# Thirty-two bytes further per k-tile: where x^T and the activations lie in SBUF, against the weight tiles

## The chip, the cores and the metric

One NeuronCore of one Trainium2 chip runs the kernel. The metric is the device time of one execution in microseconds; the median of three runs is used.

## The reference

Two transformer blocks run one after the other on 256 tokens of width 2048, all in float32. What matters here is that almost all the work lies in products of 256 token rows with large weight matrices:

```python
def first_block(x, ...):
    h = rmsnorm(x, pre_mix_g);  proj = h @ w_in            # 2048 x 4368
    ...                                                    # windowed and forgetting attention
    x = x + rmsnorm(concat([o_a, o_b]) @ w_out, post_mix_g)
    h = rmsnorm(x, pre_ffn_g);  u = causal_dwconv(h @ w_up, conv_w, conv_b)   # 2048 x 11264
    gate, val = split(u)
    return x + rmsnorm((gelu(gate) * val) @ w_down, post_ffn_g)               # 5632 x 2048

def second_block(x, c, ctx, ...):
    sh_a, sc_a, g_a, sh_m, sc_m, g_m = split(silu(c) @ w_ada + b_ada)
    ...                                                    # attention over latents and context, pooling
    x = x + g_a * (concat([attn, pool]) @ w_out)
    hm = modulate(rms_norm(x, norm_mlp_w), sh_m, sc_m)
    x = x + g_m * (square(relu(hm @ w_mlp_up)) @ w_mlp_down)                  # 2048 x 8192 x 2048
    return rms_norm(x, final_norm_w)
```

## The kernel before

Every large product is a `Group`: its weights stream from HBM in blocks of two 128-row tiles of 1024 columns (1 MB), and x^T stays in SBUF. To keep float32 accuracy, each operand is split into a high part and the rest, and each product of tiles is made of three matmuls, wh·xh, wh·xl and wl·xh (`products`, L273 to L286). ScalarE makes the high weights from the raw block (L156) and VectorE the low ones (L168), one tile of each for every 128 rows.

There are two layouts. In a feature-major product ("A": up, mup, qk, qa, q, kva, part of ckv and kv) the weight tile is the stationary operand, 128 columns at a time, and x^T of one k-tile (128 features by 256 tokens) moves. In a token-major product ("B": mdn, dn, wo_a, wo_b, wo_p, u, v) x^T of one k-tile and one token tile is stationary, and the weights move, 512 columns at a time. Names in the profile: `b_up` is the PSUM bank of an up product, `hi` and `lo` are weight tiles, `a` and `p` are x^T or activations out of the pools `a8` and `p4`.

`run` (L121 to L266) goes through the blocks in order. For each k-tile (a "unit") it issues all column tiles of that k-tile: 8 column tiles by 3 matmuls, 24, in an A product, and 4 banks by 3, 12, in a B product. The last block of a group goes bank by bank instead, alternating between its two k-tiles. So inside a unit the k-tile of x and the pair of weight buffers stay the same.

The tiles come from pools. The pool `w` has four buffers for high weights and four for low ones, 1040 columns (4160 bytes) each, used in turn. 4160 is 16·256 + 64, so the four buffers start at different places modulo 256 bytes: in the built program at 192, 0, 64 and 128, the high and the low tile of a unit alike. Pool `a8` (8 buffers of 8192 bytes) holds x^T, eight k-tiles of 256 columns per buffer (`make_ht`, L340 on), and pool `p4` (9 buffers of 4096 bytes) holds the activations of the feed-forwards, four k-tiles per buffer (L954 and L1334). A k-tile is 1024 bytes, so every k-tile starts at 192 modulo 256. Column offsets inside a weight tile are multiples of 512 bytes. The start of SBUF is taken by a scratch of 16384 bytes for DMA descriptors.

```python
            passes = ((wh, xh), (wh, xl), (wl, xh))
            for m, (ww, xx) in enumerate(passes):
                if op[0] == "A":
                    _, o, c = op
                    dst, lhsT, rhs = bank[:, o:o + 256], ww[:, c:c + 128], xx
                else:
                    _, o, w_, tt, c = op
                    dst, lhsT, rhs = bank[:, o:o + w_], xx[:, 128 * tt:128 * tt + 128], ww[:, c:c + w_]
```

Of the kernel before, what the change touches and what calls it, by code (L numbers as in the profile page):

```python
# [15 lines left out]
T = 256  # L16
# [5 lines left out]
# columns of the packed per-feature vectors  # L22
# [9 lines left out]
# when the adaptive modulation takes a step, by product: every so many ticks (99: never), or at these ticks  # L32
# [4 lines left out]
# products without a reader while the norms before these products run  # L37
# [3 lines left out]
class Group:  # L41
    """One weight-streaming product: blocks of two 128-row weight tiles against a resident x^T."""
# [10 lines left out]
def a_banks(nf, col0=0):  # L53
    """Feature-major results: two 128-feature tiles of 256 tokens per bank."""
    return [[("A", 256 * j, col0 + 128 * (i + j)) for j in range(min(2, nf - i))] for i in range(0, nf, 2)]


def b_banks(widths, col0=0):
    """Token-major results: one bank per token tile and column chunk."""
    out = []  # L60
    for tt in range(2):
        c = col0
        for n in widths:
            out.append([("B", 0, n, tt, c)])
            c += n
    return out


class Kernel:
# [51 lines left out]
    def run(self, groups):  # L121
# [26 lines left out]
        def hi_to(j):  # L148
            while len(his) <= min(j, 2 * len(blocks) - 1):
                dma_to(len(his) // 2 + 2)  # L150
                views, raw, w = part(len(his))
                self.n += 1
                hi = self.w_p.tile([128, 1040], F32R, tag="hi", name=f"hi{self.n}")[:, :w]
                with self.behind("hi"):
                    for h, r in views(hi, raw):
                        nc.scalar.copy(h, r)  # L156
                his.append(hi)

        def lo_to(j):
            while len(los) <= min(j, 2 * len(blocks) - 1):  # L160
                n = len(los)
                hi_to(n)
                views, raw, w = part(n)
                self.n += 1
                lo = self.w_p.tile([128, 1040], F32R, tag="lo", name=f"lo{self.n}")[:, :w]
                with self.behind("lo"):
                    for (l, r), (h, _) in zip(views(lo, raw), views(his[n], raw)):
                        self.dve.tensor_tensor(out=l, in0=r, in1=h.bitcast(F32), op=ALU.subtract)  # L168
                los.append(lo)

        banks = None
        for i, (g, b) in enumerate(blocks):
# [40 lines left out]
            if g.tail and b == g.nb - 2:  # L213
                # the first token tile's results come before the second's
                w2 = []
                for u in range(4):
                    lo_to(2 * i + u)
                    hi_to(2 * i + 3)
                    w2.append((his[2 * i + u], los[2 * i + u]))
                    for n in range(nb // 2):  # L220
                        unit(banks[n], g.banks[n], u)
                    self.tick(False)
                for n in range(nb):
                    if n >= nb // 2:
                        for u in range(4):
                            unit(banks[n], g.banks[n], u)
                    mm = self.mm
                    g.done(n, banks[n])
                continue
# [38 lines left out]
    def behind(self, kind):  # L268
        """Issue order after an instruction of a norm that the next products wait for."""
        q = self.held[kind]  # L270
        return self.tc.issue_after(q.pop(0).ins) if q else nullcontext()
# [31 lines left out]
    def later(self, *steps, every=1):  # L303
        """Run steps one by one at coming ticks."""
        def gen():
            for f in steps:
                for _ in range(every):
                    yield
                f()
        self.sides.append(gen())  # L310

    def keep_warm(self, n, after=None, rhs=None):
        """Products without a reader, so that the tensor engine's clock stays up while it would wait."""
# [6 lines left out]
    def preload(self, func, after):  # L320
        """Has the scalar engine load the table of a function ahead of its use."""
# [9 lines left out]
    def loader(self, w, k0, c0, n):  # L331
        """Blocks of two k-tiles from row k0 and columns c0:c0+n."""
# [7 lines left out]
    def make_ht(self, src, gain, shift=None):  # L340
        """src(tt, k) -> token-major [128, 128]; gain, shift: per-feature columns."""
# [4 lines left out]
        def emit(i):  # L346
            if len(his) <= i // 4:
                his.append(self.A8([128, 8, 256], F32R))
                los.append(self.A8([128, 8, 256], F32R))
# [32 lines left out]
        def head(tt):  # L382
            """The first four k-tiles of one token tile."""
            if not his:
                his.append(self.A8([128, 8, 256], F32R))
                los.append(self.A8([128, 8, 256], F32R))
# [15 lines left out]
    def rstd(self, parts, n):  # L402
        """(mean of squares + eps) ** -0.5 from partial sums [128, m]."""
# [14 lines left out]
    def scale_rows(self, x, ss, n=D, out=None, first=False):  # L418
        """x * rstd for a token tile; the first of two on one engine, else shared by two."""
# [12 lines left out]
    def row(self, src):  # L432
        """A vector of D on every partition, in two tiles; returns columns of it."""
# [6 lines left out]
    def attn1(self, jobs, v_of, evac, bias, sink):  # L440
        """jobs: (q, k, j, half, head). Yields once per head."""
# [87 lines left out]
    def o_evac(self, his, los, gain, acc, base=0):  # L529
        """o^T of a head pair: times the group's gain, split, and its squares summed."""  # L530
# [16 lines left out]
    def token_rstd(self, acc, n):  # L547
        """rstd per token [128, 2] from squares summed feature-major [128, 256]."""
# [49 lines left out]
    def row_of(self, cols, tile_=None):  # L598
        """A [128, 2048] tile whose every row is the vector held in columns [128, 16]."""
# [13 lines left out]
    def main(self):  # L613
# [15 lines left out]
        heads = self.const("heads", [128, 48])  # L629
# [29 lines left out]
        # x^T of the first block, one token tile after the other  # L659
# [19 lines left out]
        def silu_rows():  # L679
            """silu of c and c_ctx, each along every partition's row."""  # L680
# [18 lines left out]
        # -- v and forget gates, token-major  # L699
# [63 lines left out]
        # -- k and v of the windowed heads  # L763
# [16 lines left out]
        # -- q of the windowed heads, heads j and j + 8 in one tile  # L780
# [19 lines left out]
        # -- q and k of the forgetting heads, with the windowed attention beside them  # L800
# [27 lines left out]
        # -- output projection: windowed heads, then forgetting heads  # L828
        w_out = a["w_out"]

        def pair_rows(w, r0, n, c0):
            """Rows of k-tile j: 64 of head j, 64 of head j + n, among 2n heads from row r0."""
# [28 lines left out]
        def residual(y, x, r):  # L861
            """x += y * r for one token tile; returns the squares' sums of the new x."""
# [8 lines left out]
        def add_norm(n, half, y, hold):  # L871
            """One result chunk of y: its squares, its gain, and then x += norm(y) and y = norm(x)."""
# [44 lines left out]
        # -- residual + norm, then x^T of the next product  # L917
# [6 lines left out]
        # -- first feed-forward  # L924
        gs = {}

        def up(g):
            def after(banks):
# [23 lines left out]
                def split(i):  # L952
                    if i == 0:
                        out[:] = [self.P4([128, 4, 256], F32R) for _ in range(2)]  # L954
# [49 lines left out]
        # context: norm, modulation and its x^T beside the last products  # L1004
# [39 lines left out]
        # -- second block: context keys and values  # L1044
# [9 lines left out]
        def split(x, his, lo):  # L1054
            """hi + lo of x [128, 512], hi by partition halves in two tiles."""
# [5 lines left out]
        def twice(c):  # L1061
            """The high parts of the keys in the other partition half too."""
# [6 lines left out]
        # -- second block: projections of the latent tokens  # L1069
# [20 lines left out]
        def rope(x, his, lo):  # L1090
            """Rotated x [128, 512] (features on partitions, 256 tokens twice), as hi (by halves in two tiles) + lo."""
# [33 lines left out]
        # -- attention over the latent window and the context  # L1125
        def attn2():
            # per half s of the heads: high parts in their own partitions, low parts in the other half
# [141 lines left out]
        # -- output projection of the second block: x += g_a * (...)  # L1269
# [51 lines left out]
        # -- second feed-forward  # L1321
# [6 lines left out]
        def up2(g):  # L1328
            def after(banks):
                gs[g] = hi, lo = [], []  # L1330

                def split(i):
                    if i % 2 == 0:
                        hi.append(self.P4([128, 4, 256], F32R))  # L1334
                        lo.append(self.P4([128, 4, 256], F32R))
# [13 lines left out]
        def finish(n, half):  # L1349
            """The gain of one chunk of the last norm, and the norm when a token tile is complete."""  # L1350
# [77 lines left out]
def arrays(inp):  # L1428
    """The inputs as the program takes them, and constants that depend on shapes alone."""
# [10 lines left out]
    # the two halves of w's columns c0:c1, side by side by 512  # L1440
# [59 lines left out]
```

## Time and profile before

| | |
|---|---|
| median of 3 runs | 2159.97 us (2158.24 to 2160.66) |
| span of the profiled execution | 2159.2 us |
| TensorE busy, matmuls | 2134.7 us, 99% |
| TensorE busy, weight loads | 1926.6 us, 89% |
| VectorE busy | 1578.7 us, 73% |
| ScalarE busy | 1076.4 us, 50% |
| HBM read | 484.90 MB, 226 GB/s over the span |

The span runs from the first to the last instruction of one profiled execution; its own time is that span, 0.8 us under the median of the other runs. Busy times of different engines overlap. Matmul records overlap one another too, since a matmul is issued while the one before it is still draining; the pace of TensorE is the distance between two starts.

### The profile page before, as it was taken

What the parts mean: (1) busy time and instruction counts of PE and PEld (TensorE: products, weight loads), DVE (VectorE), ACT (ScalarE), POOL (GpSimd) and SP (SyncE); (2) the same over time, 40 slices, a digit from 0 to 9 for tenths busy, and PEclk for the clock granted to TensorE, in tenths of its full rate; (3) what the DMA queues carried; (4) which work ended last, traced back from release to release, by engine and by line L of the source; (5) the groups of instructions that cost most, each with busy time, mean ns of one, the idle gap of its engine ahead of it and who ended that gap; (6) DMA issues with size and microseconds to landing.
All of it is one profiled execution on the core that took longest, in us unless ns stands there. A gap on an engine that the chain in (4) does not pass through costs nothing.

```text
span 2159.2 us, 35018 instructions
## 1 busy us (share of the span) xinstructions
PE 2134.7 (99%) x14342; PEld 1926.6 (89%) x14342; DVE 1578.7 (73%) x2094; ACT 1076.4 (50%) x1557; POOL 38.3 (2%) x58
## 2 busy tenths in 40 slices
PE   8999999999999999999999999999999999999998
PEld 7988877999998999989889878889898998989986
DVE  6777688888689787887899777765656657555476
ACT  5456565555454543544666466354543434434343
POOL 0001010000000000000000000000000000000000
PEclk9999999999999999999999999999999999999999
DMA  8753675667767788787878744855767677565572
GB/s 309 262 191 123 157 230 218 231 244 248 254 216 254 252 298 309 273 310 255 307 259 287 247 139 156 196 175 177 252 200 270 215 246 243 191 194 179 194 233 98
DMA packets 120640, 490.86 MB, mean 227 GB/s; under 512 B 8672, under 2 KB 12576, under 8 KB 107040
## 3 DMA queue, kind: packets, MB, share of 16 engines
q1 hardware_dynamic: 120480, 488.63, 67.0%
q8 instruction: 112, 1.84, 0.3%
q14 instruction: 48, 0.39, 0.0%
HBM read 484.90 MB, written 2.13 MB: 226 GB/s over the span
## 4 chain that ended last, share of the span: by engine, by line
PE 95%; DVE 2%; ACT 1%; DMA 1%; POOL 0%; issue 0%; POOLq 0%; ACTq 0%; SPq 0%; DVEq 0%
PE b_up L285 23%; PE b_mup L285 17%; PE b_mdn L285 16%; PE b_dn L285 11%; PE b_qk L285 4%; PE b_wo_a L285 4%; PE b_u L285 2%; PE b_v L285 2%; PE b_wo_p L285 2%; PE b_qa L285 2%; PE b_q L285 2%; PE b_wo_b L285 2%; PE b_aux L1156 1%; PE b_aux L1199 1%; PE b_aux L1185 1%; PE b_aux L495 1%
## 5 line engine op out<-in xcount | busy, mean ns | idle before, releaser
L168 DVE TENSOR_TENSOR lo<-raw,hi 128x1024 fp32r<-128x1024 f32 (+2 forms) x716 | 850.0, 1198 | 445.7 <-ACT hi L156 444.2
L156 ACT CAST hi<-raw 128x1024 fp32r<-128x1024 f32 (+2 forms) x716 | 729.7, 1029 | 859.8 <-PE b_up L285 218.9
L285 PE MATMUL b_up<-a,hi 128*128 128x256 f32 x2816 | 493.9, 280 | 0.0
L285 PEld LDWEIGHTS b_up<-a,hi 128*128 128x128 f32 x2816 | 430.8, 189 | 0.4
L285 PE MATMUL b_up<-a,lo 128*128 128x256 f32 x1408 | 392.8, 279 | 0.0
L285 PE MATMUL b_mup<-a,hi 128*128 128x256 f32 x2048 | 358.8, 279 | 1.3 <-ACT a L370 1.3
L285 PE MATMUL b_mdn<-hi,p 128*128 128x512 f32 x1024 | 319.9, 393 | 0.0
L285 PEld LDWEIGHTS b_mup<-a,hi 128*128 128x128 f32 x2048 | 312.8, 189 | 2.1 <-ACT a L370 1.6
L285 PE MATMUL b_mup<-a,lo 128*128 128x256 f32 x1024 | 285.4, 279 | 0.0
L285 PEld LDWEIGHTS b_up<-a,lo 128*128 128x128 f32 x1408 | 266.1, 189 | 0.0
L583 DVE SCALAR_TENSOR_TENSOR raw<-raw,srow 128x2048 f32<-128x2048 f32 x96 | 219.4, 2286 | 28.5 <-DMA raw<-in_w_ada 28.3
L285 PEld LDWEIGHTS b_mdn<-hi,p 128*128 128x128 f32 x1024 | 191.7, 188 | 44.2
L285 PE MATMUL b_dn<-hi,p 128*128 128x512 f32 x704 | 220.1, 394 | 0.0
L285 PE MATMUL b_mdn<-lo,p 128*128 128x512 f32 x512 | 201.3, 393 | 0.0
L285 PEld LDWEIGHTS b_mup<-a,lo 128*128 128x128 f32 x1024 | 193.4, 189 | 0.0
L285 PEld LDWEIGHTS b_dn<-hi,p 128*128 128x128 f32 x704 | 131.5, 188 | 30.1
L285 PE MATMUL b_dn<-lo,p 128*128 128x512 f32 x352 | 138.5, 393 | 0.0
L285 PEld LDWEIGHTS b_mdn<-lo,p 128*128 128x128 f32 x512 | 96.3, 188 | 22.2
L285 PE MATMUL b_qk<-a,hi 128*128 128x256 f32 x512 | 94.0, 285 | 0.0
L285 PE MATMUL b_wo_a<-hi,a 128*128 128x512 f32 x256 | 81.1, 398 | 0.0
L285 PEld LDWEIGHTS b_qk<-a,hi 128*128 128x128 f32 x512 | 78.2, 189 | 2.6 <-issue 2.0
L285 PEld LDWEIGHTS b_dn<-lo,p 128*128 128x128 f32 x352 | 66.2, 188 | 15.6 <-DVE lo L168 0.4
(264 smaller groups left out, 2542.0 us busy)
## 6 DMA issues: line engine op xcount, KB each, us to landing
raw<-in_w_ada SPq DMA_DIRECT2D x96, 1024.0 KB, 5.6
raw<-in_w_up SPq DMA_DIRECT2D x88, 1024.0 KB, 5.0
raw<-in_w_mlp_up SPq DMA_DIRECT2D x64, 1024.0 KB, 5.1
raw<-in_w_mlp_down SPq DMA_DIRECT2D x64, 1024.0 KB, 5.7
raw<-in_w_in SPq DMA_DIRECT2D x50, 1024.0 KB, 6.0
raw<-in_w_down SPq DMA_DIRECT2D x44, 1024.0 KB, 6.2
raw<-in_w_out SPq DMA_DIRECT2D x32, 512.0 KB, 6.8
raw<-in_w_out SPq DMA_DIRECT2D x16, 1024.0 KB, 6.1
```

Source lines behind the costliest of these rows:

```text
L156: nc.scalar.copy(h, r)
L168: self.dve.tensor_tensor(out=l, in0=r, in1=h.bitcast(F32), op=ALU.subtract)
L285: self.mm = self.pe.matmul(dst, lhsT, rhs, start=first and n == 0 and m == 0, stop=last and n == len(prog) - 1 and m == 2, skip_group_chec ...
L495: self.pe.transpose(t[:, 128 * m:128 * m + 128], z[:, 1 + 128 * m:129 + 128 * m], self.ident)
L583: self.dve.scalar_tensor_tensor(out=r, in0=r, scalar=1.0, in1=self.srow[0], op0=ALU.mult, op1=ALU.mult, accum_out=self.ada[:, f:f + 1])
L1156: self.pe.matmul(bk[:, 256 * m:256 * m + 256], x, k[:, 512 * m + o:512 * m + o + 256], start=n == 0 and m == 0, stop=n == 1 and m == 1, sk ...
L1185: self.pe.transpose(bk[:, 128 * m:128 * m + 128], z[:, 128 * m:128 * m + 128], self.ident)
L1199: self.pe.matmul(o[64 * s:64 * s + 64, 128 * qt:128 * qt + 128], v[:, c:c + 64], PT[x][:, 128 * kt:128 * kt + 128], start=kt == 0, stop=kt ...
```

## The change

Weight tiles are allocated with 1088 columns instead of 1040 (4352 bytes, 17·256), so that all eight buffers start at the same place modulo 256. Two helpers allocate x^T and the feed-forward activations with 264 columns per k-tile instead of 256, of which 256 are used: k-tile j of a buffer then starts 32·j bytes past a multiple of 256. A buffer of `a8` becomes 8448 bytes, one of `p4` 4352. `heads` gets 16 columns more, which brings what is allocated behind it to multiples of 128 and 256. The descriptor scratch shrinks from 16384 to 1024 bytes, which makes the room. In the built program all weight tiles and all buffers of `a8` and `p4` then start at 0 modulo 256. The x tiles of the output projections (`st["oa"]`, `st["ob"]`, `st["at"]`, `st["pool"]`) are still allocated as eight adjacent k-tiles. No instruction changes its place on any engine; the writes of two k-tiles at a time (L370, L371, L956, L957, L1342, L1343 of before) become two runs of 256 columns instead of one of 512. Comments and docstrings are gone as well.

```diff
-                hi = self.w_p.tile([128, 1040], F32R, tag="hi", name=f"hi{self.n}")[:, :w]
+                hi = self.w_p.tile([128, 1088], F32R, tag="hi", name=f"hi{self.n}")[:, :w]
...
-                lo = self.w_p.tile([128, 1040], F32R, tag="lo", name=f"lo{self.n}")[:, :w]
+                lo = self.w_p.tile([128, 1088], F32R, tag="lo", name=f"lo{self.n}")[:, :w]
...
+    def xt_tile(self):
+
+        return self.A8([128, 2112], F32R).rearrange("p (k t) -> p k t", t=264)[:, :, 0:256]
+
+    def act_tile(self):
+
+        return self.P4([128, 1088], F32R)[:, :1056].rearrange("p (k t) -> p k t", t=264)[:, :, 0:256]
...
-                his.append(self.A8([128, 8, 256], F32R))
-                los.append(self.A8([128, 8, 256], F32R))
+                his.append(self.xt_tile())
+                los.append(self.xt_tile())
...
-        heads = self.const("heads", [128, 48])
+        heads = self.const("heads", [128, 64])[:, 0:48]
...
-                        out[:] = [self.P4([128, 4, 256], F32R) for _ in range(2)]
+                        out[:] = [self.act_tile() for _ in range(2)]
...
-                        hi.append(self.P4([128, 4, 256], F32R))
-                        lo.append(self.P4([128, 4, 256], F32R))
+                        hi.append(self.act_tile())
+                        lo.append(self.act_tile())
...
-    nc = bacc.Bacc("TRN2", target_bir_lowering=False, num_devices=1)
+    nc = bacc.Bacc("TRN2", target_bir_lowering=False, num_devices=1, dynamic_dma_scratch_size=1024)
```

## Rows read from the trace of the kernel before

**Rows 1.** The page: busy time, granted clock by slices, chain by engine.

```profile
PE 2134.7 (99%) x14342; PEld 1926.6 (89%) x14342; DVE 1578.7 (73%) x2094; ACT 1076.4 (50%) x1557; POOL 38.3 (2%) x58
...
PEclk9999999999999999999999999999999999999999
...
PE 95%; DVE 2%; ACT 1%; DMA 1%; POOL 0%; issue 0%; POOLq 0%; ACTq 0%; SPq 0%; DVEq 0%
```

**Rows 2.** Groups by line and shape, TensorE; busy us, mean ns of one record.

```profile
L285 PE MATMUL b_up<-a,hi 128*128 128x256 f32 x2816 | 493.9, 280 | 0.0
...
L285 PE MATMUL b_mup<-a,hi 128*128 128x256 f32 x2048 | 358.8, 279 | 1.3 <-ACT a L370 1.3
L285 PE MATMUL b_mdn<-hi,p 128*128 128x512 f32 x1024 | 319.9, 393 | 0.0
...
L285 PE MATMUL b_dn<-hi,p 128*128 128x512 f32 x704 | 220.1, 394 | 0.0
```

**Rows 3.** Timeline of TensorE in `up6`: start us, length, instruction.

```profile
736.93 0.40 PE L285 MATMUL b_up<-a,hi 128*128 128x256 f32 x2
...
739.81 0.39 PE L285 MATMUL b_up<-a,hi 128*128 128x256 f32 x2
...
742.54 0.39 PE L285 MATMUL b_up<-a,hi 128*128 128x256 f32 x2
...
745.38 0.40 PE L285 MATMUL b_up<-a,hi 128*128 128x256 f32 x2
...
745.73 0.39 PE L285 MATMUL b_up<-a,hi 128*128 128x256 f32 x2
...
746.07 0.39 PE L285 MATMUL b_up<-a,hi 128*128 128x256 f32 x2
...
748.11 0.40 PE L285 MATMUL b_up<-a,hi 128*128 128x256 f32 x2
```

**Rows 4.** Timeline of TensorE, start of `dn40`.

```profile
781.65 0.63 PE L285 MATMUL b_dn<-hi,p 128*128 128x512 f32 x2
...
783.03 0.61 PE L285 MATMUL b_dn<-hi,p 128*128 128x512 f32 x2
...
784.39 0.63 PE L285 MATMUL b_dn<-hi,p 128*128 128x512 f32 x2
...
787.19 0.62 PE L285 MATMUL b_dn<-hi,p 128*128 128x512 f32 x2
...
789.98 0.62 PE L285 MATMUL b_dn<-hi,p 128*128 128x512 f32 x2
...
792.74 0.39 PE L285 MATMUL b_dn<-hi,p 128*128 128x512 f32 x1
```

**Rows 5.** Four stretches of Rows 3: length, each engine busy, clock, DMA share, GB/s.

```profile
736.93:739.81 2.88, 2.88 (x26) 2.88 (x25) 2.78 (x6) 2.88 (x6) 0.00 (x0) 1.00 0.50 203
739.81:742.54 2.73, 2.73 (x27) 2.73 (x25) 2.73 (x4) 2.30 (x4) 0.00 (x0) 1.00 0.24 29
742.54:745.38 2.83, 2.83 (x26) 2.83 (x25) 2.83 (x6) 1.62 (x2) 0.00 (x0) 1.00 0.88 347
745.38:748.11 2.73, 2.73 (x26) 2.73 (x25) 2.63 (x6) 2.44 (x4) 0.00 (x0) 1.00 0.67 174
```

**Rows 6.** Groups by line and shape, ScalarE: weight copy, activation copy, strided copy.

```profile
L156 ACT CAST hi<-raw 128x1024 fp32r<-128x1024 f32 x668 | 694.8, 1048 | 828.3 <-PE b_up L285 218.9 <-PE b_mup L285 184.4 <-PE b_mdn L285 177.6
...
L1342 ACT CAST p<-p 128x512 fp32r<-128x512 f32 x32 | 19.7, 620 | 11.3 <-DVE p L1340 11.1
...
L395 ACT CAST a<-p 128x512 fp32r<-128x512 f32 x2 | 1.2, 622 | 0.6 <-DVE p L394 0.5
```

**Rows 7.** The page: the DMA queues.

```profile
q1 hardware_dynamic: 120480, 488.63, 67.0%
q8 instruction: 112, 1.84, 0.3%
q14 instruction: 48, 0.39, 0.0%
```

More of the change, by code (lines that the diff above doesn't have):

```diff
@@ L384, in head @@
             if not his:
-                his.append(self.A8([128, 8, 256], F32R))
-                los.append(self.A8([128, 8, 256], F32R))
+                his.append(self.xt_tile())
+                los.append(self.xt_tile())
             bk = self.bank()
```

## The prediction

> **What bounds the kernel now.** I read the page first: TensorE is busy 99% of the span, its granted clock shows 9 in every one of the forty slices, and 95% of the chain that ended last is TensorE [rows 1]. So the time is the number of matmuls times the distance from one matmul's start to the next; the other engines and the DMAs count only if they fall behind. The record lengths of the groups (279 to 280 ns for 256 moving columns, 393 to 394 ns for 512) overlap each other and are not that distance [rows 2]; it has to be taken from start times.
>
> The timeline gives it. Placement is known from the program: before, x^T and the activations start at 192 past a multiple of 256 bytes, and the four buffers for weight tiles lie at 192, 0, 64 and 128. In `up6` the buffers come in the order 192, 128, 64, 0, each read by 24 matmuls of the same shape, and the starts are 736.93, 739.81, 742.54, 745.38 and 748.11 us [rows 3]. That is 2.88, 2.73, 2.84 and 2.73 us, or **120.0, 113.8, 118.3 and 113.8 ns** per matmul. Nothing else follows this order: granted clock 1.00 in all four, VectorE busy 2.63 to 2.83 us, ScalarE 1.62 to 2.88, DMA share 0.24 to 0.88, and the two equal stretches have DMA shares of 0.24 and 0.67 [rows 5]. What differs between the four is only where the stationary operand lies against the moving one. I call d the distance (x minus weight) modulo 256: d = 0 gives 120.0, 64 gives 113.8, 128 gives 118.3, 192 gives 113.8. Mean 11.18 us / 96 = 116.5 ns.
>
> In the token-major products x is the stationary operand and the weight moves, 512 columns. In `dn40` the same four buffers take 2.74, 2.80, 2.79 and 2.76 us for 12 matmuls each [rows 4]: d = 0 gives 228.3, 64 gives 233.3, 128 gives 232.5, 192 gives 230; mean 11.09 us / 48 = 231.0 ns. The unit with d = 0 starts slow and settles: its last six matmuls take 784.39 − 783.03 = 1.36 us, 226.7 ns each. The d = 192 unit of `up6` does the same: 0.35 us for its first three (745.38 to 745.73), then 0.34 (745.73 to 746.07) [rows 3].
>
> **The change part by part.** The order of instructions on each engine stays the same. After the change every weight tile lies at 0 and k-tile j of x^T at 32·j, so d = 32·j (j is k modulo 8 for x^T, modulo 4 for activations).
>
> *Feature-major matmuls, 256 columns.* The program has 9120 of them (up 4224, mup 3072, and qk, qa, q, kva, ckv and kv together 1824; of up and mup, two in three read the high weights and one the low: x2816 and x2048 in [rows 2]). Half of them now have d = 0, 64, 128, 192 in equal parts, as all have today: 4560 at 116.5 ns, change 0. The other 4560 have d = 32, 96, 160, 224, which no row shows. Bounds from the nearest rows: 113.8 and 120.0 ns. Each of these distances has one quiet neighbour (64 or 192) and one disturbed one (0 or 128). I take the quiet value, 113.8, because where the rows show a unit change its pace inside the unit, it goes from disturbed to quiet: d = 192 here, d = 0 in `dn40`. Gain 4560 × (116.5 − 113.8) = **12.3 us**; the bounds are 12.3 us gained and 4560 × 3.5 = 16.0 us lost.
>
> *Token-major matmuls.* There are 3552 of 512 columns (mdn 1536, dn 1056, wo_a, wo_b and wo_p 768, u 192). The 768 of the output projections keep unpadded x tiles, so d = 0 for all; mdn and dn give a quarter each to d = 0, 32, 64, 96; u an eighth to each of the eight. So 1440 have d = 0, 672 each 32, 64 and 96, and 96 the rest (480 narrower ones, in v, ckv and kv, are too few to carry a term). For d = 0 I take 227.5, between the whole unit's 228.3 and the settled 226.7: 1440 × 3.5 = 5.0 us gained. For d = 64 the row gives 233.3: 672 × 2.3 = 1.5 us lost. For 32 and 96 the bounds are 226.7 and 233.3 (−5.8 to +3.1 us for 1344); I take the mean, 231.0. Sum **−3.5 us**.
>
> *The rest.* Writes of two k-tiles become two runs of 256 columns instead of one of 512: 78 on ScalarE and 78 on VectorE. A copy into four runs takes 622 ns, one into a single run 620 [rows 6], so this is below 0.5 us in all, on engines that are busy 50% and 73% [rows 1]. If the weight copies (1048 ns, two per block [rows 6]) were the bound this cover would be gone; a block of 48 matmuls takes 5.6 us, so it is not. The smaller scratch serves DMAs issued by GpSimd; all queues of this run are the hardware one and instruction fetch [rows 7], so it costs nothing and only makes room.
>
> Sum: −15.8 us of TensorE time; with TensorE 95% of the chain, −15.0. The profiled span is 2159.2 us and the median of the runs 2159.97, 0.8 more; I apply the change to the median: **2145 us**.
>
> **The rivals.**
>
> *Nothing happens between the known points (no change).* If the unseen distances lie halfway between neighbours, the 256-column term is 4560 × (116.5 − 116.5) = 0 and only −3.5 us is left: 2157 us. For it: the four known distances are spread evenly already, and a shift that visits all of them evenly has the same mean. Against it: paces inside a unit jump rather than blend. The Trainium skill, in "TensorE: Matmul & The Clock Gate", Part 2, step 1, says TensorE has two independent read ports, so that loading the next weights takes no bandwidth from the running matmul; by that rule placement would not matter at all and the time would stay at 2160 us. The trace speaks against it, 120.0 beside 113.8 ns for one shape at one clock [rows 3, 5], but it would give the same verdict as this rival.
>
> *Half-steps of 32 disturb (slower).* If a distance that is not a multiple of 64 keeps the two read streams out of step without ever settling, the odd k-tiles run like the disturbed neighbours, (120.0 + 118.3)/2 = 119.2 ns: 4560 × 2.7 = 12.3 us lost; 32 and 96 at 233.3 add 3.1, the other token-major term gives back 3.5: +11.9 us, at 95% +11, so **2171 us**. For it: d = 128 never settles in its 24 matmuls, and d = 0 stays at 120.0 throughout [rows 3]. It decides once the odd k-tiles' mean exceeds about 117.3 ns (4560 × 0.8 = 3.5, which eats the token-major gain). At the bound of 120.0 the end is 2175.
>
> *Half-steps are better than quiet.* 256 columns at the full clock of 2.4 GHz would be 106.7 ns, and 113.8 may itself contain conflicts that exist only because every operand today starts at a multiple of 64. If odd k-tiles ran midway, at 110.2, this term would be 28.7 us instead of 12.3, and with 32 and 96 of the token-major ones at 226.7 (5.8 more) the time would be about 2124 us. Nothing in the rows shows a pace below 113 ns held, so it is unlikely.
>
> **How the numbers follow.** Forecast (odd steps quiet) 0.44, its own range 2138 to 2152. The blend: 0.21, about 2157. No effect of placement at all, 2160: 0.05. Disturbed: 0.22, 2163 to 2175. Better than quiet: 0.08. The range that leaves out two in ten reaches from 2128 to 2172. A measurement here can tell about 0.2% (4.3 us) from no change. Faster takes the forecast, the better case and the lower edge of the blend: 0.44 + 0.08 + 0.06 = 0.58; slower the disturbed case, 0.22; the rest, 0.20, is within 0.2%.
>
> **What would show it.** In `up6` after the change the units follow k, not the weight buffer: k-tiles 0 and 8 should stay at 2.88 us for 24 matmuls, 2 and 6 (and 10, 14) at 2.73, 4 and 12 near 2.84, and the odd ones at 2.73 if the forecast is right, 2.80 by the blend, 2.86 by the disturbed case, 2.65 by the better one. In `dn40` the first k-tile should run near 226.7 ns throughout and the third at 233.3. VectorE's and ScalarE's groups should keep their counts and means. The prediction is wrong in its basis if the even k-tiles do not repeat today's four paces: then it was the absolute position that mattered, not the distance.

## The result and the profile after

The changed kernel takes **2171.01 us** (median of 4 runs, 2170.38 to 2172.5) beside 2160.31 for the kernel before on the same chip (4 runs, 2158.24 to 2160.92). The ratio is 1.0051 [1.0039, 1.0063]: half a per cent slower, where 0.7% faster was forecast.

The page of the changed kernel, with busy times, granted clock by slices and the chain by engine, shows the same picture as [rows 1]; its span is 2170.7 us:

```profile
PE 2145.8 (99%) x14342; PEld 1940.9 (89%) x14342; DVE 1580.5 (73%) x2094; ACT 1076.9 (50%) x1557; POOL 39.3 (2%) x58
...
PEclk9999999999999999999999999999999999999999
...
PE 95%; DVE 2%; DMA 2%; ACT 1%; issue 0%; POOL 0%; POOLq 0%; ACTq 0%; SPq 0%; DVEq 0%
```

TensorE's matmul records grew by 11.1 us (2134.7 to 2145.8) and the span by 11.5 (2159.2 to 2170.7). The other engines kept their times and the clock is at its upper level in all slices. So the loss lies in the pace of the matmuls. The groups by line and shape (busy us, mean ns of one, idle before) show which:

```profile
L285 PE MATMUL b_up<-a,hi 128*128 128x256 f32 x2816 | 500.6, 281 | 0.0
...
L285 PE MATMUL b_mdn<-hi,p 128*128 128x512 f32 x1024 | 320.3, 394 | 0.0
```

The 2816 up matmuls hold 500.6 us of records where they held 493.9 [rows 2]; the token-major ones of mdn did not move (320.3 and 319.9). On ScalarE the weight copy takes 1049 ns (1048 before), and the activation copy into two runs takes 619 (620 into one before) [rows 6].

The timeline of TensorE in `up6` (start us, length us, instruction; each row is the first of a unit of 24 matmuls) gives the paces:

```profile
739.76 0.40 PE L285 MATMUL b_up<-a,hi 128*128 128x256 f32 x2
...
742.63 0.40 PE L285 MATMUL b_up<-a,hi 128*128 128x256 f32 x2
...
745.46 0.40 PE L285 MATMUL b_up<-a,hi 128*128 128x256 f32 x2
...
748.29 0.40 PE L285 MATMUL b_up<-a,hi 128*128 128x256 f32 x2
...
751.16 0.40 PE L285 MATMUL b_up<-a,hi 128*128 128x256 f32 x2
...
754.01 0.40 PE L285 MATMUL b_up<-a,hi 128*128 128x256 f32 x2
...
756.83 0.40 PE L285 MATMUL b_up<-a,hi 128*128 128x256 f32 x2
...
759.55 0.40 PE L285 MATMUL b_up<-a,hi 128*128 128x256 f32 x2
...
762.39 0.40 PE L285 MATMUL b_up<-a,hi 128*128 128x256 f32 x2
```

From one start to the next, divided by 24, this is 119.6, 117.9, 117.9, 119.6, 118.8, 117.5, 113.3 and 118.3 ns for d = 0, 32, 64, 96, 128, 160, 192 and 224. In [rows 3] d = 64 took 113.8. Of eight units one is quiet; before, two of four were. The start of `dn40`, in the same view, twelve matmuls of 512 columns to a unit:

```profile
785.11 0.62 PE L285 MATMUL b_dn<-hi,p 128*128 128x512 f32 x2
...
787.84 0.62 PE L285 MATMUL b_dn<-hi,p 128*128 128x512 f32 x2
...
790.63 0.63 PE L285 MATMUL b_dn<-hi,p 128*128 128x512 f32 x2
...
793.43 0.62 PE L285 MATMUL b_dn<-hi,p 128*128 128x512 f32 x2
...
796.24 0.62 PE L285 MATMUL b_dn<-hi,p 128*128 128x512 f32 x2
```

That is 227.5, 232.5, 233.3 and 234.2 ns for d = 0, 32, 64 and 96, beside 228.3 and 233.3 for d = 0 and 64 in [rows 4].

The same over the whole trace: the table has the mean distance between two successive starts in the large products, without distances above 135 ns (256 columns) and 255 ns (512), which hold a wait or a missing record. All paces below are such means; some 9020 and 3440 distances enter each kernel's.

| ns from start to start | all | d = 0 | 32 | 64 | 96 | 128 | 160 | 192 | 224 |
|---|---|---|---|---|---|---|---|---|---|
| before, 256 columns | 116.5 | 119.9 | | 113.8 | | 118.1 | | 114.3 | |
| after, 256 columns | 118.1 | 119.7 | 118.0 | 117.9 | 119.5 | 118.8 | 117.5 | 115.7 | 118.2 |
| before, 512 columns | 231.4 | 229.0 | | 233.3 | | 232.6 | | 230.8 | |
| after, 512 columns | 230.7 | 227.8 | 232.6 | 232.8 | 232.7 | | | | |

The sum closes: 9120 matmuls by 118.14 − 116.51 ns are 14.9 us lost, 3552 by 230.71 − 231.41 are 2.5 gained. The difference, 12.4, at the chain's 95% is 11.8 us; measured were 10.7.

The 115.7 at d = 192 is a mean of two paces. Over `up` and `mup`, k-tile 6, a whole unit, runs at 113.9 ns; k-tile 14 lies in the last block, where two k-tiles alternate every six matmuls, and runs at 117.2.

### The profile page after: what moved, and what is told of

Same layout as the page of the kernel before. It is cut to its first block, busy times and chain, and to the rows that moved or that the text cites. A ratio compares the mean times of both kernels' runs of the same rounds, so it can differ in the third digit from the quotient of the medians.

```text
span 2170.7 us, 35018 instructions
## 1 busy us (share of the span) xinstructions
PE 2145.8 (99%) x14342; PEld 1940.9 (89%) x14342; DVE 1580.5 (73%) x2094; ACT 1076.9 (50%) x1557; POOL 39.3 (2%) x58
## 4 chain that ended last, share of the span: by engine, by line
PE 95%; DVE 2%; DMA 2%; ACT 1%; issue 0%; POOL 0%; POOLq 0%; ACTq 0%; SPq 0%; DVEq 0%
PE b_up L285 23%; PE b_mup L285 17%; PE b_mdn L285 16%; PE b_dn L285 9%; PE b_qk L285 4%; PE b_wo_a L285 4%; PE b_u L285 2%; PE b_qa L285 2%; PE b_q L285 2%; PE b_wo_p L285 2%; PE b_v L285 2%; PE b_wo_b L285 2%; PE b_aux L1164 1%; PE b_ckv L285 1%; PE b_kv L285 1%; PE b_aux L1207 1%
## 5 line engine op out<-in xcount | busy, mean ns | idle before, releaser
L285 PE MATMUL b_up<-a,hi 128*128 128x256 f32 x2816 | 500.6, 281 | 0.0
L285 PE MATMUL b_mup<-a,hi 128*128 128x256 f32 x2048 | 364.0, 281 | 1.3 <-ACT a L378 1.3
L285 PE MATMUL b_mdn<-hi,p 128*128 128x512 f32 x1024 | 320.3, 394 | 0.0
```

The costliest lines, as they stand in the source:

```text
L285: self.mm = self.pe.matmul(dst, lhsT, rhs, start=first and n == 0 and m == 0, stop=last and n == len(prog) - 1 and m == 2, skip_group_chec ...
```

## The experiments

The question is why the even k-tiles, at distances that the kernel before has too, run slower than there. Theories: (1) the pace is set by the distance modulo 256 alone; (2) what costs is that x moves by a step of 32 bytes from unit to unit; (3) absolute positions count; (4) a placement can have two paces, and what ran before chooses. Every edit is made to the changed kernel, so the small scratch is in all. As in the prediction, d is x minus weight modulo 256; a pace of 113 to 115 ns for 256 columns is called quiet. `w`, `x` and `act` stand below for where weight tiles, k-tiles of x^T and k-tiles of activations start modulo 256; products of the output projections keep x at 0 unless said. An edit shown for `hi` is made to `lo` too; e9 moves `lo` alone. Times are medians, ratios are to the kernel before.

### Distance zero throughout, and the old weight tiles

```diff
# e1_x_at_0
-    def xt_tile(self):
+    def xt_tile(self, i=0, lo=0):
+        o, p = ((0, 256), (0, 256))[lo]
+        o += 0 * i
+        t = self.A8([128, 2112], F32R)[:, o:]
+        return t[:, :8 * p].rearrange("p (k t) -> p k t", t=p)[:, :, 0:256]
...
+    def act_tile(self, lo=0):
+        o, p = ((0, 256), (0, 256))[lo]
# e2_old_weights: the padding of 264 is kept, in both pools of w
-                hi = self.w_p.tile([128, 1088], F32R, tag="hi", name=f"hi{self.n}")[:, :w]
+                hi = self.w_p.tile([128, 1040], F32R, tag="hi", name=f"hi{self.n}")[:, :w]
```

In the first, `o` is the offset in 4-byte columns and `p` the width of a k-tile; the later edits change these two. The first puts every operand at 0; the second has steps in x and in w.

> The changed kernel with its weight tiles (all at 0 modulo 256) but x^T and the activations without the padding, so every k-tile is at 0 too and the distance d is 0 for every matmul. Theory P (the pace of a matmul depends on where its two operands lie): 256-column matmuls at 119.8 ns, 512-column ones at 227.5 ns; against the kernel before 9120 x (119.8 - 116.5) = +30 us and 3552 x (227.5 - 231.4) = -14 us, so about 2176 us. Theory S (the loss of the change comes from its two-run writes, the moved buffers or the smaller scratch, and the pace per matmul has its usual mean): taking the padding away gives about 2160 us.

Measured: **2177.04 us**, 1.008 [1.0066, 1.0094]; 119.94 ns and 227.06 ns. Its groups, beside [rows 2]:

```profile
L285 PE MATMUL b_up<-a,hi 128*128 128x256 f32 x2816 | 508.6, 283 | 0.0
...
L285 PE MATMUL b_mdn<-hi,p 128*128 128x512 f32 x1024 | 315.5, 389 | 0.0
```

Without any step of x it is slower still, so the step of 32 bytes is not what costs by itself. Of the four distances in [rows 3, 4], 0 is the worst for 256 columns and the best for 512, as they showed. The sum holds again: 9120 × 3.43 = 31.3 us lost, 3552 × 4.35 = 15.5 gained, 15.8 in all, 15.0 at 95%, measured 16.7.

> The changed kernel with the padded x^T and activations, but weight tiles of 1040 columns as before, whose four buffers lie at 0, 192, 128 and 64 in turn. The distances d are the same eight, equally often, as in the change, at other absolute positions. Theory P with the distance alone: 256-column matmuls at 118.1 ns in the mean as in the changed kernel, about 2171 us. Theory P with absolute positions counting: another mean, anywhere between 113.6 and 120 ns, 2134 to 2188 us. Theory S: 2171 us, since the writes, the moves and the scratch are those of the change.

Measured: **2171.24 us**, 1.0053 [1.0037, 1.0068]; 117.86 ns and 231.39 ns. In this kernel and in the one before some units have x at 192 and w at 128, the same pair of positions. Before they take 113.8 ns, here 117.6. In `up6` of e2 this is k-tile 6, from its start to that of k-tile 7, 2.83 us for 24:

```profile
757.01 0.40 PE L285 MATMUL b_up<-a,hi 128*128 128x256 f32 x2
...
759.84 0.40 PE L285 MATMUL b_up<-a,hi 128*128 128x256 f32 x2
```

So neither distance nor position alone gives the pace: theories 1 and 3 do not suffice, and theory 4 comes up.

### All distances in steps of 16, and one distance throughout

```diff
# e3_scan16: k-tile j at 16*j
+        o, p = ((0, 260), (0, 260))[lo]
+        o += 32 * i
# e4_x192_act0: x 192, act 0, w 0
+        o, p = ((48, 256), (48, 256))[lo]
# e5_x112_act0: x 112, act 0, w 0
+        o, p = ((28, 256), (28, 256))[lo]
```

> The changed kernel with k-tile j of x^T (j = 0 to 15) at 16*j bytes, all sixteen positions modulo 256, against weight tiles at 0: one look that gives the pace of 256-column units of 24 for each position. Theory P: the values seen so far return (0: 119.8, 32: 118, 64: 118, 96: 119.4, 128: 118.8, 160: 117.4, 192: 113.6, 224: 118.1) and the unseen ones lie between 113 and 121; the time about 2171 us if the unseen ones have the mean of the seen. A rival, that only 192 is quiet because it is where streams meet no conflict: 176 and 208 are quiet too or near it. Theory S: all positions alike.

Measured: 2170.35 us in a single run. For d = 0, 16, ..., 240: 119.6, 119.0, 116.8, 118.3, 117.4, 119.9, 119.9, **113.8**, 118.5, 118.7, 117.4, 119.2, 114.1, 119.3, 118.4, 118.1 ns. Only 112 and 192 are quiet, and d = 64 is again at 117.4.

> The changed kernel without padding, x^T at 192 in every k-tile and the activations at 0, weight tiles at 0: d = 192 for all 256-column matmuls and d = 0 for nearly all 512-column ones, the two quiet pairs. Theory P: 9120 x (113.7 - 116.5) = -25.5 us and 3360 x (227.3 - 231.4) = -13.8 us against the kernel before, so about 2121 us, if nothing else becomes the bound. Theory S: about 2160 us, as the padding is gone.

Measured: **2150.08 us**, 0.9957 [0.9944, 0.9969], where 2121 was expected. The 512-column matmuls are at 226.9 ns. Those of 256 columns have two paces at one and the same placement: 113.6 ns in kva, 117.8 in qa and q, 117.7 in mup, 117.0 in up. The timeline of TensorE shows the jump between kva and qa:

```profile
64.83 0.41 PE L285 MATMUL b_kva<-a,hi 128*128 128x256 f32 x2
...
67.57 0.39 PE L285 MATMUL b_kva<-a,hi 128*128 128x256 f32 x2
...
75.74 0.29 PE L741 MATMUL b_aux<-p,p 128*128 128x16 f32 x2
...
76.97 0.48 PE L285 MATMUL b_qa<-a,hi 128*128 128x256 f32 x2
...
85.76 0.40 PE L285 MATMUL b_qa<-a,hi 128*128 128x256 f32 x2
...
88.59 0.40 PE L285 MATMUL b_qa<-a,hi 128*128 128x256 f32 x2
```

In kva 24 matmuls take 2.74 us. Then come ten small matmuls of five other lines (75.74 to 76.97), and a unit of qa takes 2.83 us for 24, at the same granted clock. Both paces are held for long.

A pause alone does the same. All of `up1` runs at 113.3 ns, and so does `up2` until, in its third unit, TensorE waits for low weights from VectorE (0.5 us in all, of which the line below shows 0.32 as idle):

```profile
467.12 0.39 PE L285 MATMUL b_up<-a,hi 128*128 128x256 f32 x2
...
469.84 0.39 PE L285 MATMUL b_up<-a,hi 128*128 128x256 f32 x2
...
470.55 0.38 PE L285 MATMUL b_up<-a,lo 128*128 128x256 f32 x1 [0.32 <-DVE lo L168]
...
473.24 0.40 PE L285 MATMUL b_up<-a,hi 128*128 128x256 f32 x2
...
476.07 0.40 PE L285 MATMUL b_up<-a,hi 128*128 128x256 f32 x2
```

The 24 matmuls before take 2.72 us, the 24 from 473.24 on 2.83, and `up3` to `up10` stay at 117.8 ns. All of these products read the same x^T and use the weight buffers in the same turn. So one placement has two paces, a pause can change one for the other, and no theory of positions alone (3), whatever the modulus, explains it.

> As the version with x^T at 192 and the activations at 0, but x^T at 112 in every k-tile: the one position of the sixteen-step scan beside 192 that ran at 113.8 ns. Theory L (a distance can have two paces, and the pace a stream of matmuls falls into depends on the matmuls before): if 112 has a slow pace as well it may be caught in it for whole products, 117 to 120 ns, 2150 us or more; if it has only the quiet one, 113.6 ns and about 2118 us. Rival A (one pace for each pair of absolute positions, 112 against 0 being quiet): 2118 us.

Measured: **2120.76 us**, 0.9818 [0.9802, 0.9835]: 1.8% faster than before and 50 us faster than the change. The group of the up matmuls and, in `up6`, the timeline:

```profile
L285 PE MATMUL b_up<-a,hi 128*128 128x256 f32 x2816 | 481.4, 276 | 0.0
```

```profile
723.95 0.39 PE L285 MATMUL b_up<-a,hi 128*128 128x256 f32 x2
...
726.67 0.39 PE L285 MATMUL b_up<-a,hi 128*128 128x256 f32 x2
...
729.39 0.39 PE L285 MATMUL b_up<-a,hi 128*128 128x256 f32 x2
```

Every unit of `up6` takes 2.72 us, 113.3 ns each. Over the trace it is 113.64 and 226.96 ns. The sum: 9120 × 2.87 = 26.2 us and 3552 × 4.45 = 15.8, at 95% 39.9; measured are 39.5 against 2160.3. Where `up0` and `mup0` still wait now and then for their x^T, the pace is back at 113.3 ns by the end of each unit with a wait. At this placement the slow pace of e4 does not hold.

### A kick between units, and the whole change moved by 64 bytes

```diff
# e6_kick, on e4: w at 32 for k-tiles 0 and 8
+        def off(j):
+            (g, b), u = blocks[j // 2], j % 2
+            return 8 if g.nk == 16 and g.kpc == 1 and (2 * b + u) % 8 == 0 else 0
...
-                hi = self.w_p.tile([128, 1088], F32R, tag="hi", name=f"hi{self.n}")[:, :w]
+                hi = self.w_p.tile([128, 1088], F32R, tag="hi", name=f"hi{self.n}")[:, off(len(his)):off(len(his)) + w]
# e7_shift64: w, x and act all 64 further, x in steps of 32 as in the change
+        o, p = ((16, 264), (16, 264))[lo]
...
+                hi = self.w_p.tile([128, 1088], F32R, tag="hi", name=f"hi{self.n}")[:, 16:16 + w]
```

> As the version with x^T at 192 and the activations at 0, but the weight tiles of k-tiles 0 and 8 of the products with sixteen k-tiles lie 32 bytes further, so that these two units have d = 160 and the other fourteen d = 192, all at the same positions as before. Theory L: the unit at 160 takes the stream out of the slow pace and the next unit settles at 113.6 ns as it does behind 160 in the changed kernel; mean (14 x 113.6 + 2 x 117.4)/16 = 114.1 ns against 117.1, 27 us less than that version: about 2123 us. Rival A (the pace belongs to the pair of positions, and 192 against 0 is 117.1 ns): the fourteen stay at 117.1, about 2150 us.

Measured: **2135.34 us**, 0.9884 [0.9869, 0.9899], half way between the two expectations of 2123 and 2150. The fourteen other k-tiles, still at x 192 and w 0, go from e4's 117.1 ns to 114.8 on average; the kicked ones take 118.5. The timeline of `up6` (four lines further down in this kernel) shows the kicked unit and two after it:

```profile
729.19 0.41 PE L289 MATMUL b_up<-a,hi 128*128 128x256 f32 x2
...
732.07 0.40 PE L289 MATMUL b_up<-a,hi 128*128 128x256 f32 x2
...
734.80 0.39 PE L289 MATMUL b_up<-a,hi 128*128 128x256 f32 x2
...
737.52 0.39 PE L289 MATMUL b_up<-a,hi 128*128 128x256 f32 x2
```

120.0, 113.8 and 113.3 ns. One unit at another placement puts most of the following ones into the quiet pace: the pace depends on what ran before.

Why only half way, the trace shows too. Behind the kick at k-tile 8 the seven next units run at 113.3 to 114.0 ns in all 19 `up` and `mup` products. Behind the kick at k-tile 0 they do so (113.4) in the seven products that follow another `up` or `mup`; in the ten that follow `dn` or `mdn` they stay at 117.8, and `up0` and `mup0`, with waits in them, are mixed. In `up7`, which follows `dn`, the unit behind the first kick takes 2.82 us:

```profile
819.44 0.40 PE L289 MATMUL b_up<-a,hi 128*128 128x256 f32 x2
...
822.26 0.40 PE L289 MATMUL b_up<-a,hi 128*128 128x256 f32 x2
```

Ten products with 7 × 24 matmuls at 4.4 ns more are 7.4 of the 12 us missing. The same edit works or fails by what ran before it.

> The changed kernel with x^T, the activations and the weight tiles all 64 bytes further: every distance in every product with padded x is the same as in the change, in the same order, only the absolute positions differ. Theory L: the same paces unit by unit (in up6 119.4, 118.0, 118.0, 119.4, 118.8, 117.4, 113.6, 118.1 ns for d = 0, 32, ..., 224), about 2172 us (the output projections, whose x tiles stay at 0, get d = 192, some 2 us more). Rival A (absolute positions count): other paces, d = 64 at 113.6 for instance as in the kernel before.

Measured: 2172.17 us in a single run, and the change's paces again within 0.1 ns at every distance (d = 64: 117.87, d = 192: 115.75). When both operands move by 64 nothing changes, so a common shift by 64 does not count. No other shift is tried here.

### Steps of 8, the low weights elsewhere, steps of 64

```diff
# e8_scan8: k-tile j at 64 + 8*j, act 0, w 0
+        o, p = ((16, 258), (16, 258))[lo]
+        o += 16 * i
# e9_low_weights: x 0, high weights 0, low weights 144
+                lo = self.w_p.tile([128, 1088], F32R, tag="lo", name=f"lo{self.n}")[:, 36:36 + w]
# e10_step64: k-tile j at 64*j, w 0
+        o, p = ((0, 272), (0, 272))[lo]
```

> x^T with k-tile j at 64 + 8*j bytes, j = 0 to 15, activations and weight tiles at 0: one look at the paces for distances 64 to 184 in steps of 8, each reached from the one 8 below. Theory L: 112 quiet again or not, depending on what 104 leaves behind; paces between 113 and 120 ns with jumps. Rival A: 64, 80, 96, 112, 128, 144, 160 and 176 repeat the values of the scan in steps of 16 (117.4, 119.9, 119.9, 113.8, 118.5, 118.7, 117.4, 119.2). The time, with the activations at d = 0, about 2157 us by both.

Measured: 2172.29 us in a single run, 15 above the 2157 expected. For d = 64, 72, ..., 184: 117.7, 120.0, 118.3, 120.0, 119.5, 127.2, **114.5**, 120.7, 118.8, 120.3, 118.8, 120.0, 117.4, 119.6, 117.8, 120.2 ns. Distances that are odd multiples of 8 are all at 119.5 or above, 112 is quiet again, and none lies under 113 ns. At d = 104 the starts lie 122 or 123 and 137 or 138 ns apart in turn, so the limit of 135 ns is left out there: 129.1 ns in 17 of the 19 `up` and `mup` products, the slowest pace of all runs.

> x^T and activations at 0, high weight tiles at 0, low weight tiles at 144, so that in the 256-column products d is 0 for wh.xh and wh.xl and 112 for wl.xh. With all at 0 every one of the three takes 120.0 ns. Theory N (the conflict is between the columns that a matmul streams and the weight load of the next matmul, which runs beside it): the matmul beside which the low weights are loaded, wh.xl, becomes the quiet one or the fastest of the three; mean about 117.8 ns. Theory O (a matmul's own two operands): wl.xh becomes the quiet one. Theory I (no interplay, the position of the weight tile alone): only records with the low tile differ. The time about 2177 - 20 = 2157 us by either of the first two, as a third of 9120 gain 6.4 ns.

Measured: 2174.72 us in a single run, 18 above the 2157 expected. The three passes of a product, wh·xh, wh·xl and wl·xh, move together: 117.5, 118.0 and 117.2 ns (e1: 119.9 in all three). The 512-column ones lose: 234.5, 232.3 and 232.3 (e1: 227.2, 227.1, 226.9). So it is not only the matmul whose own weight lies elsewhere that changes. Whether a matmul is slowed by the load of its own weights or of the next ones, this run does not tell apart: it is inconclusive there.

> The change with steps of 64 bytes instead of 32: k-tiles at 0, 64, 128, 192, 0, ... against weight tiles at 0, so that the distances come in the order of the kernel before (0, 64, 128, 192) and the odd multiples of 32 are gone. Theory L (distance and what runs before): the paces of the kernel before, 120.0, 113.5, 118.2, 114.1 ns, mean 116.5, and only the 768 matmuls of the output projections gain, 3 us: about 2157 us. Rival A (absolute positions, 64 against 0 at 118 ns as in the changed kernel): 2280 x 4.4 = 10 us more, about 2167 us.

Measured: **2169.97 us**, 1.0051 [1.0034, 1.0068], where 2157 was expected if the 32-byte distances were the fault. Here there are none left, only d = 0, 64, 128 and 192 in the order in which the kernel before has them, and the time is that of the change. The timeline of TensorE in `up6`:

```profile
737.58 0.39 PE L285 MATMUL b_up<-a,hi 128*128 128x256 f32 x2
...
740.44 0.40 PE L285 MATMUL b_up<-a,hi 128*128 128x256 f32 x2
...
743.27 0.40 PE L285 MATMUL b_up<-a,hi 128*128 128x256 f32 x2
...
746.11 0.40 PE L285 MATMUL b_up<-a,hi 128*128 128x256 f32 x2
...
748.94 0.40 PE L285 MATMUL b_up<-a,hi 128*128 128x256 f32 x2
```

119.2, 117.9, 118.3 and 117.9 ns; over the trace 119.5, 117.5, 118.7 and 116.4. The two quiet units of [rows 3] are gone here, but not everywhere. In the ten `up` and `mup` products that follow `dn` or `mdn`, the first unit at d = 64 takes 113.6 ns and the first at 192 takes 113.8, and the later ones 118.0 and 117.8 in whole units. In `up7`, k-tile 1:

```profile
830.27 0.40 PE L285 MATMUL b_up<-a,hi 128*128 128x256 f32 x2
...
833.00 0.39 PE L285 MATMUL b_up<-a,hi 128*128 128x256 f32 x2
```

That is 113.8 ns for the step of x that ends at 117.9 in `up6`.

### The same distances made by the weights

```diff
# e11_weights_move: x 0, act 0; w 0, 192, 128, 64
+        o, p = ((0, 256), (0, 256))[lo]
...
+                hi = self.w_p.tile([128, 1040], F32R, tag="hi", name=f"hi{self.n}")[:, :w]
```

This has the distances and their order as e10, but x stays and the weight tile moves from unit to unit.

> The changed kernel with x^T and activations unpadded at 0 and weight tiles of 1040 columns, whose buffers lie at 0, 192, 128, 64 in turn: the distances come as 0, 64, 128, 192, the order of the version with steps of 64 bytes, but it is the weight tile that moves from unit to unit, as in the kernel before, and not x. The smaller scratch, the moved buffers and the changed constants of the change are all in it. Theory L2 (distance, and the way in which a unit is entered: a step of the weight tile ends in the quiet pace at d = 64 and 192, a step of x in the slow one): the paces of the kernel before, 120, 113.5, 118.2, 114.1 ns, and 2160 us. Rival A (absolute positions): x at 0 is a new set of pairs, 113 to 120 ns each, and a time between 2140 and 2180 us. Theory S (scratch, moved buffers): about 2170 us, as in the change.

Measured: **2160.44 us**, 1.0003 [0.9994, 1.0013], and the paces of the kernel before to 0.2 ns: 119.9, 113.8, 118.1 and 114.4 ns, 231.4 for 512 columns. The same view of `up6`:

```profile
736.86 0.40 PE L285 MATMUL b_up<-a,hi 128*128 128x256 f32 x2
...
739.74 0.39 PE L285 MATMUL b_up<-a,hi 128*128 128x256 f32 x2
...
742.47 0.39 PE L285 MATMUL b_up<-a,hi 128*128 128x256 f32 x2
...
745.30 0.40 PE L285 MATMUL b_up<-a,hi 128*128 128x256 f32 x2
...
748.04 0.40 PE L285 MATMUL b_up<-a,hi 128*128 128x256 f32 x2
```

120.0, 113.8, 117.9 and 114.2 ns. In what TensorE reads, e10 and e11 differ in which operand steps between units, and with it in the positions, and they differ by 9.5 us. A step of the weight tile ends in the quiet pace at d = 64 and 192, a step of x only in some places (e10). e11 also shows that the smaller scratch and the 16 columns of `heads` cost nothing, since both are in it.

### Does the distance do it in the better version?

```diff
# e12_d112_shifted: x 192, act 80, w 80 (d = 112 and 0)
+        o, p = ((48, 256), (48, 256))[lo]
...
+                hi = self.w_p.tile([128, 1088], F32R, tag="hi", name=f"hi{self.n}")[:, 20:20 + w]
# e13_best_shift64: x 176, act 64, w 64, x of the output projections 64
+        o, p = ((44, 256), (44, 256))[lo]
...
+                hi = self.w_p.tile([128, 1088], F32R, tag="hi", name=f"hi{self.n}")[:, 16:16 + w]
```

> The version with x^T at 112 and weight tiles at 0, moved as a whole: weight tiles and feed-forward activations at 80, x^T at 192. The distance stays 112 in the 256-column products and 0 in mdn and dn; the output projections' x tiles stay at 0, so their 768 matmuls get d = 176. Distance theory: 256-column matmuls at 113.6 ns again, about 2121 us, up to 4 us more for the output projections. Rival A (absolute positions): x^T at 192 against 80 is a new pair, 113.6 to 121 ns, 2121 to 2188 us.

Measured: **2184.6 us**, 1.0117 [1.0102, 1.0133], the slowest of all, with e5's distances: 119.5 ns, and 230.9 where activations and weights both lie at 80 (e5: 227.0). The output projections, whose x stays at 0, have d = 176 here. The group, beside 481.4 us in e5:

```profile
L285 PE MATMUL b_up<-a,hi 128*128 128x256 f32 x2816 | 507.2, 283 | 0.0
```

This is not e5's placement caught in a second pace by a pause: no unit of `up` or `mup` runs under 118 ns, those with waits in `up0` and `mup0` included, where e5 comes back to 113.3.

> The version with x^T at 112 and everything else at 0, moved as a whole by 64 bytes: weight tiles, activations and the x tiles of the output projections at 64, x^T at 176. Moving it by 80 brought 119.5 ns where 113.6 had stood. Theory M (the pattern repeats when both operands move by 64, since what counts is the distance modulo 256 and each start modulo 64): 113.6 ns and 226.9 ns again, 2121 us. Rival A (absolute positions modulo 256): any pace between 113 and 121 ns, 2121 to 2190 us.

Measured: **2121.86 us**, 0.9825 [0.9809, 0.9841]; 113.62 and 226.98 ns, e5 again:

```profile
L285 PE MATMUL b_up<-a,hi 128*128 128x256 f32 x2816 | 481.7, 276 | 0.0
```

Moving e5 by 64 bytes keeps its paces, moving it by 80 loses them. So where the operands start modulo 64 counts beside the distance modulo 256. A common shift by 32 was not tried, so modulo 32 would fit as well.

## Why the prediction was wrong

**The basis held.** TensorE's pace is the time: with the counts of the prediction, the measured paces give the measured times to 1 or 2 us for the change, e1 and e5. That placement changes the pace at one and the same clock is confirmed far beyond the rows it was read from: 2177 us (e1) and 2121 us (e5) are the same instructions, with x^T 112 bytes further in one. As the prediction reads the rule in "TensorE: Matmul & The Clock Gate" of the Trainium skill, Part 2, step 1, all of these would take one time; the runs speak against that by 56 us.

**"4560 at 116.5 ns, change 0" failed.** The even k-tiles run at 118.0: 4560 × 1.5 = 6.8 us lost, 4.7 of them at d = 64 (1140 × 4.1). The prediction took each distance to own a pace, from the units of `up6`. Elsewhere the kernel before shows the second pace too. In its `up0` k-tile 7, d = 192, takes 2.47 us for 21 matmuls, 117.6 ns each:

```profile
398.48 0.40 PE L285 MATMUL b_up<-a,hi 128*128 128x256 f32 x2
...
400.95 0.40 PE L285 MATMUL b_up<-a,hi 128*128 128x256 f32 x2
```

All its steps are steps of the weight tile, and behind these the quiet pace is the rule at d = 64 and 192. In the change x steps and the weight stays; d = 64 then stays at 117.9, and d = 192 is quiet in whole units only (113.9, else 117.2). What the runs show in place of one pace per distance: one placement can have two paces, and what ran or paused before it decides (e2, e4, e6). Which operand steps is part of that (e10, e11), but not all: in e10 the same step of x ends in either pace.

**"I take the quiet value, 113.8" for the odd k-tiles failed.** They run at 118.3: 4560 × 1.8 = 8.2 us lost instead of 12.3 gained. The argument from units that settle inside themselves was an argument from two units; none of the four odd distances settles in the change.

**The token-major term was right**: 2.5 us gained, 3.5 forecast. d = 0 is at 227.8 (227.5 taken), 64 at 232.8 (233.3), and 32 and 96 at 232.6 and 232.7, near the upper bound instead of the mean of 231.0. **The rest was right**: copies into two runs take 619 ns (620 into one), and e11 has the scratch at no cost.

**The rivals.** The disturbed case gave 2171, and 2171 it is, with odd tiles at 118.3 (119.2 there) above its deciding point of 117.3. That the number agrees is luck: it had 12.3 us lost at the odd k-tiles and none at the even ones, the runs show 8.2 and 6.8, and e10, without any odd distance, loses as much. And the reading "then it was the absolute position that mattered" is not what follows from the even tiles: e7 moves all positions by 64 and changes nothing. What the runs leave standing is distance modulo 256 together with the starts modulo 64 (or 32), and at some placements two paces, chosen by what ran or paused before.

**Open.** Why this is so is not settled. That the loading of weights meets the stream of moving columns is an argument from the paces' dependence on both operands' places; e9 did not tell whose load. A kernel without weight loads between matmuls was not tried.

## What to carry to other kernels

Where TensorE is the bound, measure the distance from start to start by the placement of moving and stationary operand, and try one common offset between them for all tiles, before spreading tiles over many offsets: here x^T at 112, with weight tiles and activations at 0, gave 1.8%, the spread lost 0.5%. A pace read for a placement in one order of work is not a property of the placement; try it in the order in which it will run, and read it over the whole trace: four units of `up6` hid the second pace. When an edit changes which operand moves between units, treat every known pace as unknown.

## What was not expected of the hardware

One placement, two paces, each held for many matmuls: x at 192 and w at 0 runs at 113.6 ns in kva and at 117.8 in qa of one execution (e4), a pause of 0.5 us is enough to go from one to the other, and one unit in eight at another placement brings most of the others back (e6, 114.8). Nothing in scans by 16 and 8 bytes goes under the quiet pace of 113.3 ns for 256 columns, and d = 104 goes up to 129.1; 512 columns take 227.0 at best. The Trainium skill, in "TensorE: Matmul & The Clock Gate", Part 1, "Wait — 56ns, not 53.3ns?", has N/2.4 GHz and about 2.5 ns from start to start, which by estimate would be 109.2 and 215.8 ns; no run here goes so low.
